# Head of a hybrid decoder step: adaLN modulation in tiles of 128 columns, a PSUM bank each for factors and shifts, low weight parts on VectorE

## The chip, the cores and the metric

One core of one Trainium2 chip runs the whole program. The metric is the time of one execution on the device in microseconds (us). Engines: TensorE (PE, with its weight loads as PEld), VectorE (DVE), ScalarE (ACT), GpSimd (POOL) and SyncE (SP), which here only issues DMAs. Each engine works through a stream of its own in the order written, and waits for other engines by semaphores.

## What is computed

One step of a decoder layer with 1024 new prompt tokens and 32 new sample tokens (8 sequences of 4). The head, where the change lies, is `modulated_input` and the first two column blocks of the product with `w_in`:

```
mod = jax.nn.silu(c) @ w_ada + b_ada
shift, scale, gate = jnp.split(mod, 3, axis=-1)
h = rms_norm(x, g_norm) * (1 + scale[:, None, :]) + shift[:, None, :]
...
u = h @ w_in
```

`c` has 9 rows (one for the prompt, eight for the samples), `w_ada` is 1024 x 3072, `w_in` 1024 x 6468. Behind the head come the remaining projections, an index with the choice of 256 keys per query, retention, sparse attention and the output projection. All products with `h` are made in split precision: an operand is cut into a high part (rounded to the PE's fast fp32 format) and a low part (the rest), and three products are summed: high by high, low of `h` by high of the weight, high of `h` by low of the weight.

## The kernel before

`h` is kept transposed: model columns on the partitions, in 8 tiles `k` of 128 columns, with 1056 tokens beside each other. `XT[:, k]` holds x transposed; `HH[k]` and `HL[k]` are the high and low parts of the modulated tile.

**Loading.** SP issues, in this order: x in nine row tiles; then for each of the `GROUPS` of one or two column tiles the scale columns and the shift columns of `w_ada` (`load_wa`, L329 to L335, 1 MB for a group of two, 512 KB for one), and behind each of the first four groups a quarter (`piece`) of the two first blocks of `w_in` (`ws`, L345). x and `w_ada` share six buffers of 1 MB (`part`, L258).

**Start.** PE transposes x (L307), ACT and DVE evacuate it and sum its squares (`x_block`), DVE makes the inverse root for all tokens in nine small steps (L438 to L446), PE spreads it over the partitions (`spreads`, L452), and ACT copies that into `RB`.

**A tile.** For each tile `k` there is a chain over the engines:
- `modulation(g, o)`, step `m` in the table: PE multiplies silu(c) by the group's `w_ada` columns (L220), in 8 products of 32 rows that fill four row groups; ACT copies the result to SBUF (L388). `o` is 1 for the scale, 0 for the shift.
- `gather(k, o)` (L397): PE sums the four row groups and turns the tile's result into columns in PSUM. All columns of both kinds stand in the tile `Z`; the results of `modulation` stand in the two halves of the tile `M`.
- `factor(k)` (ACT, L406) makes `AA`, the factor of the tile; `scaled(k, 0)` and `scaled(k, 1)` (DVE, L409) multiply the prompt's two halves of `XT[:, k]` by it and by `RB`; `new_scaled` (L412) does it for the 32 sample tokens. This is `scale_tile`, step `z.1`.
- `moved(k)` (ACT, L418) makes `BB`, the shift; `new_moved` (DVE, L415) adds it for the samples; `high(k, 0)`, `high(k, 1)` (ACT, L421) write `HH[k]` with the shift added; `low` (DVE, L424) writes `HL[k]`. This is `shift_tile`, step `z.0`.
- `weight_high` (ACT, L427) and `weight_low` (POOL, L430) split a piece of the two weight blocks; a piece serves two tiles.
- `products` (PE, L243): five matmuls (three of 352 columns, two of 400) for each of the terms 0 (high by high), 1 (low of `h`) and 2 (low of the weight).

The order of all this is written by hand. `on` (L355) ties each instruction behind the one written before it on its engine, and the table `steps` says which pieces of work stand between the terms of each tile:

```
steps = {0: "0 2 1 m21", 1: "0 z21 m20 1a z20 1b 2 m31", 2: "0 z31 1 m30 2a z30 2b", 3: "0 z41 z40 1 2 m51",
         4: "0 z51 m50 1a z50 1b 2", 5: "0 z61 z60 1 2 m71", 6: "0 z71 m70 1a z70 1b 2", 7: "0 1 2"}
```

The factor and the shift of tiles 0 and 1 come ahead of the first product, and tile 1 is modulated before the loop. `idle` (L368) puts matmuls of zeros on PE while it would stand still there. Behind the head the next blocks follow at L227 to L229 (`terms`), with weights split at L212 (ACT) and L213 (DVE, every third on POOL). `prefetch` loads their weights (L206) into the buffers of `ws`, once these are split.

Of the kernel before, what the change touches and what calls it, by code (L numbers as in the profile page):

```python
# [125 lines left out]
def _hybrid_step(ctx, tc, A, outs, dbg):  # L126
# [124 lines left out]
    Z, M = pt(), pt()  # L251
    with ExitStack() as s0:
# [23 lines left out]
        X, pair = {}, [None]  # L276

        def x_load(i):
            t = SEQ[i]
            if i % 2 == 0:  # L280
                pair[0] = part()
            X[t] = pair[0][:, i % 2]
# [93 lines left out]
        rows_, group, turn = {}, {}, [0]
        for g, n in GROUPS:
            group.update({k: g for k in range(g, g + n)})

        def modulation(g, o):  # L380

            n = dict(GROUPS)[g]
            at = 256 * (turn[0] % 2)
            pm = M[:, at:at + 128 * n]
            pe(lambda: ada_rows(pm, lambda c: wa[g, o][:, c]))
            ar = rows_[g, o] = BI[(5, 6, 3, 4)[turn[0] % 4]].bitcast(F32)[:, :128 * n]
# [1 line left out]
            return lambda: sca.copy(ar, pm)  # L388
# [4 lines left out]

        def gather(k, o):

            at = 128 * (k - group[k])
            pe(lambda: nc.tensor.matmul(column(k, o), rows_[group[k], o][:, at:at + 128], C[:, C_S9 + 9 * (1 - o):C_S9 + 9 * (1 - o) + 9], start=True, stop=True))  # L397
# [49 lines left out]
        spread = [pj(), px().rearrange("p a b -> p (a b)")]  # L447

        def spreads(g):
            for o in range(4):  # L450
                i = 1 + 4 * g + o
                last = nc.tensor.matmul(spread[g][:, 128 * o:128 * o + 128], y[:, i:i + 1].to_broadcast([128, 128]), ident, start=True, stop=True)  # L452
            return last

        dve(*held[6:])
# [2 lines left out]
        pe(lambda: spreads(0), lambda: nc.tensor.matmul(own, y[:NS, 0:1].to_broadcast([NS, 128]), ident[:NS, :NS], start=True, stop=True))
        gather(0, 1)
        gather(1, 1)  # L460
        act(lambda: sca.copy(RB[:, :512], spread[0]), factor(0), factor(1))
        pe(lambda: spreads(1))
        act(lambda: sca.copy(RB[:, 512:T], spread[1]))
# [2 lines left out]
        W = [[sp.tile([128, KT, 128], F32R, name="w", bufs=4) for _ in "hl"] for _ in (0, 1)]
        pe(idle(6, 256, spare))
        kept = modulation(0, 0)
        act(kept)
        pe(idle(4, 256, spare))  # L470
        gather(0, 0)
        gather(1, 0)
        pe(idle(8, 256, spare))
        act(moved(0))
        dve(new_moved(0))
        act(weight_high(0, 0), high(0, 0), weight_high(1, 0))
        pool(weight_low(0, 0), weight_low(1, 0))
        dve(lambda: vec.tensor_scalar(HH[0][:, parts[1]], XT[:, 0, parts[1]], shift(0), None, op0=OP.add),
            low(0, 0), low(0, 1))
# [1151 lines left out]
```

## Time and profile before

| what | us |
| --- | --- |
| median of three runs (lowest, highest) | 1107.62 (1106.94, 1108.46) |
| the profiled execution's own time | 1108.76 |
| its span, first to last instruction | 1107.0 |
| DVE busy, ACT busy, POOL busy in the span | 677.0, 468.9, 238.0 |
| first product of the head (L243) starts | 26.07 |
| first product behind the head (L227) starts | 63.61 |

A page of the profile gives the busy time of each engine, lists the costliest groups of instructions, and says what ended the idle time before them. Further views are cut from the same trace: the timeline (start, duration, engine, line, operation, output and input tiles, and in brackets how long the engine had been idle before and what released it), the waits (who waited for whom, in all, how often, longest), stretches of time with the busy time of each engine, and the DMA traffic of a stretch. PEld rows show when PE took up a matmul, which is sharper than the modelled ends of PE rows.

### The profile page before, as it was taken

What the parts mean: (1) busy time and instruction counts of PE and PEld (TensorE: products, weight loads), DVE (VectorE), ACT (ScalarE), POOL (GpSimd) and SP (SyncE); (2) the same over time, 40 slices, a digit from 0 to 9 for tenths busy, and PEclk for the clock granted to TensorE, in tenths of its full rate; (3) what the DMA queues carried; (4) which work ended last, traced back from release to release, by engine and by line L of the source; (5) the groups of instructions that cost most, each with busy time, mean ns of one, the idle gap of its engine ahead of it and who ended that gap; (6) DMA issues with size and microseconds to landing.
All of it is one profiled execution on the core that took longest, in us unless ns stands there. A gap on an engine that the chain in (4) does not pass through costs nothing. (4 is left out here: it accounts for less than half of the span.)

```text
span 1107.0 us, 20368 instructions
## 1 busy us (share of the span) xinstructions
PE 1085.6 (98%) x8081; PEld 986.4 (89%) x8081; DVE 677.0 (61%) x1626; ACT 468.9 (42%) x919; POOL 238.0 (21%) x203
## 2 busy tenths in 40 slices
PE   7999999999999999999999999999999999999996
PEld 6789889899999989999999998887998888898775
DVE  6685348698877878999233222210357767497665
ACT  5475445554554554333244233311336656342111
POOL 0213006113311311020422222244114333000000
PEclk9999999999999999999999999999999999999998
DMA  9643435164344516432886867476798520466431
GB/s 328 189 110 97 122 98 156 47 205 138 92 132 136 175 37 191 142 95 88 287 285 204 239 172 246 130 279 229 256 318 297 182 69 30 138 190 246 160 117 57
DMA packets 149956, 185.63 MB, mean 168 GB/s; under 512 B 18644, under 2 KB 120932, under 8 KB 148772
## 3 DMA queue, kind: packets, MB, share of 16 engines
q1 hardware_dynamic: 139488, 147.81, 42.2%
q0 software_dynamic: 9856, 35.66, 9.8%
q8 instruction: 63, 1.03, 0.4%
q10 hardware_dynamic: 516, 0.86, 0.2%
q14 instruction: 33, 0.27, 0.1%
HBM read 139.34 MB, written 41.17 MB: 163 GB/s over the span
## 5 line engine op out<-in xcount | busy, mean ns | idle before, releaser
L227 PE MATMUL pj<-hh,wh 128*128 128x352 f32 (+1 forms) x1168 | 382.7, 328 | 0.0
L228 PE MATMUL pj<-hl,wh 128*128 128x352 f32 (+1 forms) x1168 | 378.7, 324 | 0.0
L229 PE MATMUL pj<-hh,wl 128*128 128x352 f32 (+1 forms) x1168 | 378.1, 324 | 0.2 <-POOL wl L213 0.2
L227 PEld LDWEIGHTS pj<-hh,wh 128*128 128x128 f32 x1168 | 219.3, 188 | 8.4 <-issue 7.1
L228 PEld LDWEIGHTS pj<-hl,wh 128*128 128x128 f32 x1168 | 219.8, 188 | 6.8 <-issue 6.0
L229 PEld LDWEIGHTS pj<-hh,wl 128*128 128x128 f32 x1168 | 219.4, 188 | 3.8 <-issue 3.2
L997 DVE TENSOR_SCALAR_CACHE_REDUCE eq<-sc,cand 128x896 bf16<-128x896 f32 (+4 forms) x155 | 135.7, 876 | 2.5
L212 ACT CAST wh<-ws 128x1024 fp32r<-128x1024 f32 (+1 forms) x65 | 61.0, 942 | 117.2 <-PE pj L228 88.0
L213 DVE TENSOR_TENSOR wl<-ws,wh 128x1024 fp32r<-128x1024 f32 (+1 forms) x47 | 52.8, 1124 | 41.6 <-ACT wh L212 41.4
L1345 POOL TENSOR_SCALAR lg<-lg,st 128x1024 f32<-128x1024 f32 (+7 forms) x64 | 47.7, 751 | 115.9 <-DVE st L1344 64.9
L213 POOL TENSOR_TENSOR wl<-ws,wh 128x1024 fp32r<-128x1024 f32 x18 | 43.3, 2405 | 93.6 <-ACT wh L212 87.6
L1343 ACT ACTIVATE lg<-lg,st 128x1024 f32<-128x1024 f32 (+7 forms) x64 | 49.4, 774 | 27.6 <-DVE st L1342 26.0
L1215 DVE COPY kt<-str 128x512 f32<-128x512 f32 x32 | 22.1, 691 | 63.3 <-PE str L1213 55.9
L1542 PE MATMUL pj<-woh,MH 128*128 128x512 f32 (+1 forms) x136 | 51.4, 378 | 0.0
L1543 PE MATMUL pj<-wol,MH 128*128 128x512 f32 (+1 forms) x136 | 51.2, 377 | 0.0
L1544 PE MATMUL pj<-woh,ML 128*128 128x512 f32 (+1 forms) x136 | 51.2, 377 | 0.0
L1182 POOL DMA_INDIRECT kv<-in_cache_k,idx x32 | 30.1, 941 | 94.4 <-PE str L1213 85.6
L1215 ACT COPY kt<-str 128x512 f32<-128x512 f32 x32 | 18.8, 588 | 61.9 <-PE str L1213 58.3
L1358 PE MATMUL tr<-C,lg 128*128 128x128 f32 x288 | 43.0, 278 | 1.5 <-ACT pT L1361 0.6
L835 ACT ACTIVATE raw<-pj 128x352 f32<-128x352 f32 x48 | 22.3, 464 | 48.3 <-PE pj L229 41.9
L1182 POOL DMA_INDIRECT kv<-in_cache_v,idx x32 | 31.5, 984 | 52.2 <-PE sx L1243 27.8
L1358 PEld LDWEIGHTS tr<-C,lg 128*128 128x128 f32 x288 | 32.5, 140 | 9.1 <-issue 4.9
(368 smaller groups left out, 1981.1 us busy)
## 6 DMA issues: line engine op xcount, KB each, us to landing
ws<-in_w_in SPq DMA_DIRECT2D x49, 512.0 KB
rot<-in_rot SPq DMA_DIRECT2D x8, 1056.0 KB
TG<-raw SPq DMA_DIRECT2D x15, 528.0 KB
x<-in_w_ada SPq DMA_DIRECT2D x6, 1024.0 KB
wst<-in_w_out SPq DMA_DIRECT2D x12, 512.0 KB
u<-TG SPq DMA_DIRECT2D x8, 528.0 KB
t<-TG SPq DMA_DIRECT2D x8, 528.0 KB
x<-in_x_prompt SPq DMA_DIRECT2D x8, 512.0 KB
```

The costliest lines, as they stand in the source:

```text
L212: nc.scalar.copy(wh[:, :, :n], ws[:, :, :n])
L213: (nc.vector if k == 4 or len(order) % 3 else nc.gpsimd).tensor_sub(wl[:, :, :n], ws[:, :, :n], f32(wh[:, :, :n]))
L227: nc.tensor.matmul(p, wh[:, k], HH[k][:, sl], start=(k == 0), stop=False)
L228: nc.tensor.matmul(p, wh[:, k], HL[k][:, sl], start=False, stop=False)
L229: nc.tensor.matmul(p, wl[:, k], HH[k][:, sl], start=False, stop=(k == KT - 1))
L997: nc.vector.tensor_scalar(junk[:n, :W], sc, thr[:n, j:j + 1], 0.0, op0=op, op1=OP.add, accum_out=cnt[:n, j:j + 1])
L1182: nc.gpsimd.indirect_dma_start(out=t.rearrange("p s c -> p (s c)"), out_offset=None, in_=cache.rearrange("g (r s) h d -> (g r) (s h d)", s ...
L1343: nc.scalar.activation(l, l, AF.Exp, bias=st[:, 2:3], scale=0.125, accum_out=st[:, 3:4])
L1358: step["turned"] = nc.tensor.transpose(x[:, 128 * (j - j0):128 * (j - j0) + 128], lg[:, j % 2, 128 * (j // 2):128 * (j // 2) + 128], ident)
L1542: nc.tensor.matmul(x, MH[:, k, tk], wh[:, k], start=(k == 0), stop=False)
L1543: nc.tensor.matmul(x, MH[:, k, tk], wl[:, k], start=False, stop=False)
L1544: nc.tensor.matmul(x, ML[:, k, tk], wh[:, k], start=False, stop=(k == KT - 1))
```

## The change

`w_ada` is loaded tile by tile in 512 KB for scale and shift each, from eleven buffers of 512 KB; a piece of `w_in` follows the tiles 0, 2, 4 and 5 (`AT`). The results and columns of the scale stand in one PSUM tile, `S[0]`, those of the shift in another, `S[1]`. Only the factor and shift of tile 0 are made ahead of the first product. In the loop both modulations of tile k+2 stand behind the terms of tile k, and scale and shift of tile k+1 directly behind each other. `weight_high` moves from `scale_tile` to `shift_tile`, and `weight_low` from POOL to DVE, behind `low`. Of the `idle` matmuls 4 of 384 columns are left; 18 of 256 go. At the start the second half of tile 0 is scaled from PSUM and not from `RB`, and the held copies of x stand in another order.

```
-GROUPS = ((0, 2), (2, 1), (3, 2), (5, 2), (7, 1))
...
-    Z, M = pt(), pt()
+    S = [pt(), pt()]
...
-        part = lambda: sp.tile([128, 2, D], F32, name="x", bufs=6)
+        part = lambda: sp.tile([128, D], F32, name="x", bufs=11)
...
-        def load_wa(g, n):
+        AT = (0, 2, 4, 5)
+
+        def load_wa(k):
             for o in (1, 0):
-                w = part().rearrange("p a b -> p (a b)")[:, :KT * 128 * n].rearrange("p (k f) -> p k f", k=KT)
-                loads.append(nc.sync.dma_start(w, wcols(A["w_ada"][0], KT, 1024 * o + 128 * g, 128 * n)))
-                wa[g, o] = w
+                w = wa[k, o] = part().rearrange("p (k f) -> p k f", f=128)
+                loads.append(nc.sync.dma_start(w, wcols(A["w_ada"][0], KT, 1024 * o + 128 * k, 128)))
...
-        for j, (g, n) in enumerate(GROUPS):
-            load_wa(g, n)
-            if j < 4:
+        for k in range(KT):
+            load_wa(k)
+            if k in AT:
+                i = AT.index(k)
...
+        def modulation(k, o):
+            pm = S[1 - o][:, :128]
+            pe(lambda: ada_rows(pm, lambda c: wa[k, o][:, c]))
+            ar = rows_[k, o] = BI[(5, 6, 3, 4)[turn[0] % 4]].bitcast(F32)[:, :128]
+            turn[0] += 1
+            act(lambda: sca.copy(ar, pm))
...
         def column(k, o):
-            return Z[:, 18 * k + 9 * (1 - o):18 * k + 9 * (1 - o) + 9]
+            return S[1 - o][:, 256 + 9 * k:265 + 9 * k]
...
         def weight_low(i, j):
-            return lambda: gps.tensor_sub(W[i][1][:, piece[j]], ws[i][:, piece[j]], f32(W[i][0][:, piece[j]]))
+            return lambda: vec.tensor_sub(W[i][1][:, piece[j]], ws[i][:, piece[j]], f32(W[i][0][:, piece[j]]))
...
-        pe(idle(4))
-        kept = modulation(0, 1)
-        act(kept)
+        spare = px().rearrange("p a b -> p (a b)")
+        pe(idle(2, spare))
+        modulation(0, 1)
+        pe(idle(2, spare))
+        gather(0, 1)
+        act(factor(0))
...
+        pe(spreads(0), lambda: nc.tensor.matmul(own, y[:NS, 0:1].to_broadcast([NS, 128]), ident[:NS, :NS], start=True, stop=True))
+        act(lambda: sca.copy(RB[:, :512], spread[0]))
+        modulation(0, 0)
+        pe(spreads(1, (0, 1)))
+        gather(0, 0)
...
+        act(weight_high(0, 0), moved(0))
...
+            scaled(0, 0, RB[:, :512]), new_scaled(0), new_moved(0))
+        pe(spreads(1, (2, 3)))
+        dve(scaled(0, 1, spread[1]))
+        act(high(0, 0), weight_high(1, 0), lambda: sca.copy(RB[:, 512:T], spread[1]))
         dve(lambda: vec.tensor_scalar(HH[0][:, parts[1]], XT[:, 0, parts[1]], shift(0), None, op0=OP.add),
-            low(0, 0), low(0, 1))
...
+            low(0, 0), low(0, 1), weight_low(0, 0), weight_low(1, 0))
+        modulation(1, 1)
...
         def shift_tile(k):
             gather(k, 0)
             act(moved(k))
             dve(new_moved(k))
+            if k in AT:
+                act(*[weight_high(i, AT.index(k)) for i in (0, 1)])
             act(high(k, 0), high(k, 1))
             dve(low(k, 0), low(k, 1))
+            if k in AT:
+                dve(*[weight_low(i, AT.index(k)) for i in (0, 1)])
...
+        steps = ["0a 0b m10 z11 1 z10 2 m21 m20"] + ["0 z%d1 z%d0 1 2 m%d1 m%d0" % (k + 1, k + 1, k + 2, k + 2) for k in range(1, 6)] + ["0a z71 z70 0b 1 2", "0 1 2"]
```

In the new table `0a` is the first of a term's five matmuls and `0b` the other four.

The start on DVE, from the root's application to the sample tokens on. Before (hh_77 and hl_85 are the parts of tile 0, hl_86 one of tile 1):

```order
L464 TENSOR_TENSOR xt<-xt,px 128x8x32
L409 SCALAR_TENSOR_TENSOR xt<-xt,AA,rb 128x512 x2
L412 TENSOR_TENSOR xt<-xt,AA 128x32
L409 SCALAR_TENSOR_TENSOR xt<-xt,AA,rb 128x512 x2
L412 TENSOR_TENSOR xt<-xt,AA 128x32
L415 TENSOR_TENSOR xt<-xt,pt 128x32
L478 TENSOR_SCALAR hh_77<-xt,BB 128x544
L424 SCALAR_TENSOR_TENSOR hl_85<-xt,BB,hh_77 128x512
L424 SCALAR_TENSOR_TENSOR hl_85<-xt,BB,hh_77 128x544
L415 TENSOR_TENSOR xt<-xt,pt 128x32
```

The same place of DVE in the changed kernel, where L401 is `scaled`, L404 `new_scaled`, L407 `new_moved`, L416 `low` and L422 `weight_low`:

```order
L462 TENSOR_TENSOR xt<-xt,px 128x8x32
L401 SCALAR_TENSOR_TENSOR xt<-xt,AA,rb 128x512
L404 TENSOR_TENSOR xt<-xt,AA 128x32
L407 TENSOR_TENSOR xt<-xt,pt 128x32
L401 SCALAR_TENSOR_TENSOR xt<-xt,AA,pj 128x512
L467 TENSOR_SCALAR hh_77<-xt,BB 128x544
L416 SCALAR_TENSOR_TENSOR hl_85<-xt,BB,hh_77 128x512
L416 SCALAR_TENSOR_TENSOR hl_85<-xt,BB,hh_77 128x544
L422 TENSOR_TENSOR w<-ws,w 128x256 x2
L401 SCALAR_TENSOR_TENSOR xt<-xt,AA,rb 128x512 x2
```

Tile 1's scaling (three rows before) has moved behind tile 0's low part, the second half of tile 0 reads PSUM (pj), and two low parts of weights stand in the row.

PE in the step of tile 6 (hh_83, hl_91), before; L220 is the shift's modulation of tile 7, L397 the gathers:

```order
L243 MATMUL pl<-hh_83,w 128x352 x2
L243 MATMUL pj<-hh_83,w 128x352
L243 MATMUL pl<-hh_83,w 128x400 x2
L397 MATMUL pt<-C,bi_99 128x9
L220 MATMUL pt<-x,scT 32x128 x8
L243 MATMUL pl<-hl_91,w 128x352 x2
L243 MATMUL pj<-hl_91,w 128x352
L397 MATMUL pt<-C,bi_100 128x9
L243 MATMUL pl<-hl_91,w 128x400 x2
```

The same step in the changed kernel, from the modulations of tile 7 (L219) behind tile 5 on:

```order
L219 MATMUL pt<-x,scT 32x128 x16
L242 MATMUL pl<-hh_83,w 128x352
L389 MATMUL pt<-C,bi_97 128x9
L389 MATMUL pt<-C,bi_98 128x9
L242 MATMUL pl<-hh_83,w 128x352
L242 MATMUL pj<-hh_83,w 128x352
L242 MATMUL pl<-hh_83,w 128x400 x2
L242 MATMUL pl<-hl_91,w 128x352 x2
L242 MATMUL pj<-hl_91,w 128x352
L242 MATMUL pl<-hl_91,w 128x400 x2
```

Both modulations of tile 7 now stand ahead of tile 6, and both gathers follow each other behind the first matmul.

More of the change, by code (lines that the diff above doesn't have):

```diff
@@ L275, in _hybrid_step, with x_load @@
         size = lambda t: 128 if t < 8 else NS
[L276 to L282, printed above, removed]
+        X = {}
+        def x_load(t):
+            X[t] = part()
             nc.sync.dma_start(X[t][:size(t)], xp[t * 128:t * 128 + 128] if t < 8 else xs)
@@ L362, in on, with idle @@
                 L[engine] = made.ins
-        pe, act, dve, pool = [lambda *fs, e=e: on(e, *fs) for e in "pavg"]
-        vec, sca, gps = nc.vector, nc.scalar, nc.gpsimd
+        pe, act, dve = [lambda *fs, e=e: on(e, *fs) for e in "pav"]
+        vec, sca = nc.vector, nc.scalar
         L["p"], L["a"], L["v"] = [last_on(e) for e in (mybir.EngineType.PE, mybir.EngineType.Activation, mybir.EngineType.DVE)]
-        def idle(n, w=384, out=M):
+        def idle(n, out):
             def run():
                 for i in range(n):
-                    last = nc.tensor.matmul(out[:, 512 - w:], zeros[:, :128], zeros[:, :w], start=True, stop=True)
+                    last = nc.tensor.matmul(out[:, :384], zeros[:, :128], zeros, start=True, stop=True)
                 return last
             return run
[L376 to L386, printed above, removed]
+        rows_, turn = {}, [0]
+        def modulation(k, o):
+            pm = S[1 - o][:, :128]
+            pe(lambda: ada_rows(pm, lambda c: wa[k, o][:, c]))
+            ar = rows_[k, o] = BI[(5, 6, 3, 4)[turn[0] % 4]].bitcast(F32)[:, :128]
             turn[0] += 1
-            return lambda: sca.copy(ar, pm)
+            act(lambda: sca.copy(ar, pm))
         def column(k, o):
-            return Z[:, 18 * k + 9 * (1 - o):18 * k + 9 * (1 - o) + 9]
+            return S[1 - o][:, 256 + 9 * k:265 + 9 * k]
         def gather(k, o):
-            at = 128 * (k - group[k])
-            pe(lambda: nc.tensor.matmul(column(k, o), rows_[group[k], o][:, at:at + 128], C[:, C_S9 + 9 * (1 - o):C_S9 + 9 * (1 - o) + 9], start=True, stop=True))
+            pe(lambda: nc.tensor.matmul(column(k, o), rows_[k, o], C[:, C_S9 + 9 * (1 - o):C_S9 + 9 * (1 - o) + 9], start=True, stop=True))
         halves = (slice(0, 512), slice(512, T))
@@ L446, in _hybrid_step @@
             lambda: vec.scalar_tensor_tensor(y, u, 1.875, y, op0=OP.add, op1=OP.mult))
[L447 to L455, printed above, removed]
-        own = px()[:, 0, :NS]
-        spare = px().rearrange("p a b -> p (a b)")
@@ L458, in _hybrid_step @@
[L458 to L463, printed above, removed]
-        dve(lambda: vec.tensor_tensor(XT[:, :, T:], XT[:, :, T:], own.unsqueeze(1).to_broadcast([128, KT, NS]), op=OP.mult),
-            scaled(0, 0, RB[:, :512]), scaled(0, 1, RB[:, 512:T]), new_scaled(0), scaled(1, 0, RB[:, :512]), scaled(1, 1, RB[:, 512:T]), new_scaled(1))
@@ L466, in _hybrid_step @@
[L466 to L478, printed above, removed]
-            low(0, 0), low(0, 1))
@@ L480, in _hybrid_step, with spreads, run @@
-        act(moved(1))
-        dve(new_moved(1))
-        act(high(1, 0), high(1, 1))
-        dve(low(1, 0), low(1, 1))
+        spread = [pj(), pj()]
+        def spreads(g, os=range(4)):
+            def run():
+                for o in os:
+                    i = 1 + 4 * g + o
+                    last = nc.tensor.matmul(spread[g][:, 128 * o:128 * o + 128], y[:, i:i + 1].to_broadcast([128, 128]), ident, start=True, stop=True)
+                return last
+            return run
+        dve(held[8], held[6], held[7])
@@ L486, in _hybrid_step @@
         ps = ps1.enter_context(tc.tile_pool(name="ps", bufs=1, reuse_waits="tile", space=PSUM))
-        Z, M = pt(), pt()
+        S[:] = pt(), pt()
         banks = first_banks()
-        def put(k, term, some=slice(None)):
-            pe(lambda: Ins(products(W, banks[some], k, term)))
         def scale_tile(k):
@@ L495, in scale_tile @@
             act(factor(k))
-            if k % 2 == 0:
-                act(*[weight_high(i, k // 2) for i in (0, 1)])
-                pool(*[weight_low(i, k // 2) for i in (0, 1)])
             dve(scaled(k, 0, RB[:, :512]), scaled(k, 1, RB[:, 512:T]), new_scaled(k))
```

24 lines of the change are left out of this document (11 added, 13 removed).

## The prediction

> **What bounds the kernel now.** I read the page first, then stretches of time.
>
> ```profile
> span 1107.0 us, 20368 instructions
> ...
> 0.00:64.00 64.00, 55.70 (x445) 44.55 (x446) 44.13 (x89) 35.57 (x79) 10.66 (x13) 0.97 0.75 240
> ...
> PE tr L1358 <- ACT pT L1361: 0.6, 2, 0.3
> ```
>
> The columns of a stretch are its length, busy time of PE, PEld, DVE, ACT and POOL, granted PE clock, DMA share and GB/s. PE is busy for 55.7 of the head's 64 us, so 8.3 of idle lie here; the last row leads the list of PE's waits for other engines behind 63.4 us. PE sets the pace there, and what the head saves should reach the end. The waits of 26 to 63.5 us say what holds PE back there:
>
> ```profile
> DVE xt L409 <- ACT AA L406: 6.2, 6, 1.9
> ACT hh L421 <- DVE xt L415: 4.3, 4, 1.3
> PEld pl L243 <- ACT hh L421: 3.1, 5, 1.0
> ...
> PE pt L397 <- ACT AA L406: 0.9, 2, 0.5
> ```
>
> No row names a DMA. PE waits for the high part, ACT for the sample tokens, DVE for the factor: the chain of a tile. Here it is for tile 7, to the head's end:
>
> ```profile
> 57.53 0.37 PEld L397 LDWEIGHTS pt<-C,bi 128*128 128x128 f32 x2
> 58.03 0.36 ACT L406 ACTIVATE AA<-pt,cols 128x9 f32<-128x9 f32 x1 [1.01 <-PE pt L397]
> 58.42 1.42 DVE L409 SCALAR_TENSOR_TENSOR xt<-xt,AA,rb 128x512 f32<-128x512 f32 x2 [0.74 <-ACT AA L406]
> 59.40 0.26 ACT L418 ACTIVATE BB<-pt,cols 128x1 f32<-128x1 f32 x1 [0.50 <-PE pt L397]
> 59.70 1.36 ACT L421 ACTIVATE hh<-xt,BB 128x512 fp32r<-128x512 f32 x2
> 60.04 0.19 DVE L415 TENSOR_TENSOR xt<-xt,pt 128x32 f32<-128x32 f32 x1
> 60.45 1.45 DVE L424 SCALAR_TENSOR_TENSOR hl<-xt,BB,hh 128x512 fp32r<-128x512 f32 x2 [0.22 <-ACT hh L421]
> 61.11 0.19 PEld L243 LDWEIGHTS pl<-hh,w 128*128 128x128 f32 x1 [0.45 <-ACT hh L421]
> 62.08 2.40 POOL L213 TENSOR_TENSOR wl<-ws,wh 128x1024 fp32r<-128x1024 f32 x1 [6.33 <-ACT wh L212]
> 63.43 0.19 PEld L227 LDWEIGHTS pj<-hh,wh 128*128 128x128 f32 x1
> ```
>
> From the gather at 57.53 to the second high part's end (59.70 + 1.36 = 61.06) pass 3.53 us, and PE takes the tile's second matmul right behind, at 61.11. Other tiles take longer:
>
> ```profile
> 29.74 0.30 PEld L243 LDWEIGHTS pl<-hh,w 128*128 128x128 f32 x2 [0.20 <-issue]
> 30.52 0.37 PEld L397 LDWEIGHTS pt<-C,bi 128*128 128x128 f32 x2
> 31.41 1.89 DVE L409 SCALAR_TENSOR_TENSOR xt<-xt,AA,rb 128x512 f32<-128x512 f32 x2 [1.47 <-ACT AA L406]
> 52.37 0.37 PEld L397 LDWEIGHTS pt<-C,bi 128*128 128x128 f32 x2
> ```
>
> The scaling takes 1.89 us, not 1.42, while POOL makes weight parts. From tile 2's gather (30.52) to tile 7's (57.53) pass 27.01 us, 5.4 a tile; from tile 6's (52.37) alone 5.16.
>
> **Part 1: the tiles' rhythm.** First PE's own work. A term of five matmuls takes 30.52 - 29.74 = 0.78 us. Two modulations of 128 columns in a row exist later, and two gathers at the start:
>
> ```profile
> 232.63 0.81 PEld L220 LDWEIGHTS pj<-ws,scT 128*32 128x32 f32 x32 [0.22 <-issue]
> 233.64 0.19 PEld L227 LDWEIGHTS pj<-hh,wh 128*128 128x128 f32 x1 [0.20 <-issue]
> ...
> 20.50 0.52 PEld L397 LDWEIGHTS pt<-C,bi 128*128 128x128 f32 x4
> 20.94 0.19 PEld L452 LDWEIGHTS px<-C,yy 128*128 128x128 f32 x1
> ```
>
> The pair takes the gap of 0.22 ahead and 233.64 - 232.63 = 1.01, so 1.23 us; the two gathers take 0.44. A tile of the new table is 3 x 0.78 + 0.44 + 1.23 = 4.01 us of PE.
>
> Now the chain with the shift's gather directly behind the scale's: gather at 0, `AA` 0.50 to 0.86, scaling 0.89 to 2.31, samples scaled and shifted by 2.70 (0.19 each, as at 60.04), second high part 2.73 to 3.45. PE takes the second matmul at about 3.5, and after four matmuls (0.63) the next tile's gather: a period of 4.15 us. The first matmul can run at 0.44 + 2 x 0.78 + 1.23 = 3.23, so PE idles some 0.1 us a tile: two limits, 4.01 and 4.15, nearly meet. The separate banks matter here: PE's two waits of L397 on `AA` (up to 0.5 us) were the shift's gather waiting for the factor's read of the shared tile `Z`.
>
> Does DVE fit? It takes 1.42 + 0.19 + 0.19 + 1.45 = 3.25 us a tile, and on four tiles the weights' low parts:
>
> ```profile
> L213 DVE TENSOR_TENSOR wl<-ws,wh 128x512 fp32r<-128x512 f32 x16 | 11.3, 712 | 0.0
> ...
> 62.98 2.57 DVE L213 TENSOR_TENSOR wl<-ws,wh 128x1024 fp32r<-128x1024 f32 x1 [0.81 <-ACT wh L212]
> ```
>
> Half of 0.712 is 0.36 for 128x256; the upper end is a quarter of the 2.57 us pass over 1024 columns, which ran beside POOL's of 62.08: 0.64. With POOL idle I take 0.36, the nearer row: 3.25 + 0.72 = 3.97 us, inside 4.15, so it costs nothing while DVE's wait for the factor covers it. At 0.64 a tile would be 4.53, up to 0.4 too long on four tiles, 1.5 us in all. ACT needs 2 x 0.27 (copies) + 0.36 + 0.26 + 1.36 = 2.5 us a tile, and its weight parts fall into its wait for the scaling. POOL's passes vanish from the loop, and with them the 1.89.
>
> So tile 2's gather to tile 7's: four periods and a last one where `0a` alone stands ahead of the gathers. There PE needs only 3.3 us, but ACT must first finish tile 6's second high part (3.45) and the copy of the factor's row (0.27): 3.75. Sum 4 x 4.15 + 3.75 = 20.35 against 27.01: **-6.65 us**.
>
> **Part 2: the start.**
>
> ```profile
> 18.57 0.17 DVE L446 SCALAR_TENSOR_TENSOR yy<-rb,yy 128x9 f32<-128x9 f32 x1
> 20.27 0.59 ACT L461 COPY rb<-pj 128x512 f32<-128x512 f32 x1 [0.69 <-PE pj L452]
> 25.36 0.72 ACT L421 ACTIVATE hh<-xt,BB 128x512 fp32r<-128x512 f32 x1
> 25.42 0.50 DVE L478 TENSOR_SCALAR hh<-xt,BB 128x544 fp32r<-128x544 f32 x1
> 26.30 1.17 PE L243 MATMUL pl<-hh,w 128*128 128x352 f32 x6
> 29.17 0.38 PEld L220 LDWEIGHTS pt<-x,scT 128*32 128x32 f32 x16 [0.26 <-issue]
> 29.88 0.27 ACT L388 COPY bi<-pt 128x128 f32<-128x128 f32 x1 [0.76 <-PE pt L220]
> ...
> L1545 DVE SCALAR_TENSOR_TENSOR xo<-pj,gb 128x512 f32<-128x512 f32 x15 | 10.2, 686 | 14.8 <-PE pj L1544 13.3 <-DMA out<-xo 1.3
> ```
>
> The root (18.74) still comes when it did, the copy into `RB` at about 20.1. The shift of tile 0 now sits on PE at 20.3: from a modulation (29.17) to its copy's end (30.15) pass 0.98 us, gather and `BB` take 0.8 (a gather's 0.50 as ahead of `AA`, and 0.26), so `BB` is there at 22.1 and the high part at 22.1 to 22.85, where it began at 25.36. The second half waits for the second spread (22.4), scaling from PSUM 0.75 (between 0.69 as in the last row, another pass from PSUM, and 0.95, half of 1.89) and DVE's high part 0.50: second matmul at 23.75 against 26.30. But four matmuls (0.63), a lone modulation (29.74 - 29.17 and a gap, 0.82), two lone gathers (0.35 each), two terms and a pair (1.23) come before tile 1: 23.75 + 0.63 + 0.82 + 0.70 + 1.56 + 1.23 = 28.7, and tile 2's gather at 29.5 against 30.52: **-1.0 us**. The removed zero matmuls stood in waits for ACT and DVE, so their going saves nothing beside that. Of the moved DVE copies, the one that frees the second spread's bank goes first; they end when they did, and cost nothing.
>
> **Part 3: the end.** PE's first low-weight matmul behind the head waited for POOL's 2.40 us (62.08), which followed ACT's split, which followed tile 7's high part: 62.08 + 2.40 = 64.48, 3.4 us behind 61.06. That tail stays.
>
> **Part 4: the loads.** Packets per 3 us with 1 KB pieces (14 to 17 us) and with 512-byte pieces (22 to 25 us), and when the first piece of `w_ada` was there:
>
> ```profile
> DMA packets 1033, 1.06 MB, mean 352 GB/s; under 512 B 16, under 2 KB 1028, under 8 KB 1033
> ...
> DMA packets 1775, 0.89 MB, mean 296 GB/s; under 512 B 52, under 2 KB 1775, under 8 KB 1775
> ...
> 18.07 0.59 PEld L220 LDWEIGHTS pt<-x,scT 128*32 128x32 f32 x16 [0.40 <-DMA x<-in_w_ada]
> ```
>
> All of `w_ada` now comes at the lower rate. At 14.0 us x, whose pieces are 4 KB, is over (1,028 of the 1,033 packets behind it are under 2 KB). From there 9.44 MB (8.39 of `w_ada`, 1.05 of `w_in`) take 31.9 us; each landing lags by 1.05 us (1.05 MB at 352 GB/s end at 17.0, PE went on at 18.07). Tile 7's shift lands at 47.0; PE wants it at 48.9 (tile 6's gather at 29.5 + 4 x 4.15 = 46.1, then 0.44, two terms, and the first of the pair). The least slack, tiles 3 and 6, is 1.3 us. The buffers cost no wait: the sixteen loads need eleven, and each later one takes that of an x tile or of a modulation long past. So the loads cost nothing, by a thin cover: 3.99 us per tile against 4.15.
>
> **Sum.** -6.65 - 1.0 = -7.65. No tile of before ran without a small stall that such a sum leaves out; I give back 0.1 a tile: **-7.0 us**. On the profiled run's 1108.76 (span 1107.0) that is 1101.8; the median of the runs is 1.1 lower: **1100.6**.
>
> **Rivals.**
>
> *A cold clock.*
>
> ```profile
> 39.40:42.80 3.40, 2.09 (x12) 1.72 (x12) 2.11 (x4) 2.24 (x6) 0.24 (x1) 1.00 1.11 300
> 42.80:46.20 3.40, 3.40 (x18) 2.55 (x20) 3.14 (x6) 1.63 (x3) 1.91 (x2) 0.53 0.09 29
> ```
>
> After a stretch with 2.09 of 3.40 us busy the clock fell to 0.53 for the next 3.4 us: 0.47 x 3.4 = 1.6 us of work lost, a part of the 27.01; the 20.35 has none such. The new start has fewer fillers; at 22.3 to 25.7 I count 2.3 us of PE work. If that, or a stall in the loop, costs one to three such stretches, the time is 1102.2 to 1105.4. The Trainium skill ("TensorE: Matmul & The Clock Gate", Part 1) says that it takes an idle window of about 3.4 us; by that no fall would come here, but the trace had one at 61% busy.
>
> *Loads set the pace.* At 270 GB/s tile 7's shift lands at 50.0, 1.1 late: 1101.7; at 250, 52.8 and 3.9 late: about 1104.5. **Slower** than before comes from the same place: tile 7's high part ends 2.7 us behind the landing (0.98 + 0.05 + 0.43 + 0.26 + 0.22 + 0.75), so the old 61.06 is missed if the landing is past 58.4, that is under 9.44 MB / 43.3 us = 218 GB/s. At 200 GB/s the landing is at 62.2: +3.8, 1111.4. For it: half as many packets again (6,144 of 12,288 are cut in two) and a slack of 1.3 us. Against: 296 GB/s on just such packets.
>
> The Trainium skill ("DMA: Bandwidth & Descriptors", sections Anatomy of one DMA and Bandwidth) speaks for this rival: batch transfers to 1 MiB or more. By the page's fit of 2.0 us plus the bytes at 436 GB/s, an estimate for sixteen loads one at a time is 51 us where the old ten need 39, and the kernel would be slower. The trace doesn't bear that out: loads of 128 and 512 KB flowed at 22 to 25 us without a gap.
>
> *It doesn't carry.* The head ends earlier, but an index load or a weight block then holds PE; against it speaks that PE's waits behind the head are tiny. 1107.6.
>
> **Chances.** Forecast (1099 to 1102.5) 0.60; cold clock or loads at 250 to 270 (to 1105.4) 0.23; no change within 0.2% (2.2 us, about what a measurement can tell) 0.09; slower 0.08, against faster 0.83. The range leaves out the last two and a bit below: 1098 (no give-back, and the high parts a little quicker) to 1106.
>
> **What would show it.** Right: tile 2's gather near 29.5, gathers 4.1 to 4.3 us apart, tile 7's second high part ending near 54, low weights of 0.36 us on DVE, no wait for `w_ada` after 18 us. Wrong: PE waiting for a DMA, a clock near 0.5, or scaling (DVE) waiting behind `low`.

## The result, and the profile after

The changed kernel takes 1100.66 us (median of 4 runs, 1099.72 to 1101.49) against 1107.28 us of the kernel before beside it (4 runs, 1106.85 to 1108.46): ratio 0.9938, 95% interval 0.9921 to 0.9956. A second set gave 1100.81 us (5 runs), ratio 0.9935, 0.9921 to 0.9948. The profiled execution has a span of 1099.7 us, 7.3 less than before.

The whole and the head's 64 us, in the columns of the prediction's stretches:

```profile
span 1099.7 us, 20540 instructions
...
0.00:64.00 64.00, 55.77 (x556) 48.37 (x557) 48.59 (x106) 41.77 (x98) 2.58 (x5) 1.00 0.83 240
```

POOL's 10.66 us have become 2.58, and the mean clock went from 0.97 to 1.00. PE's waits of 26 to 57.5 us, out of the list of waits:

```profile
DVE xt L401 <- ACT AA L398: 4.8, 6, 1.6
...
PEld pt L219 <- DVE hl L416: 1.3, 1, 1.3
PE pt L219 <- DVE hl L416: 1.1, 1, 1.1
...
PEld pl L242 <- ACT hh L413: 0.9, 3, 0.5
```

The waits of L397 (now L389) on `AA` are gone; a wait of a modulation, L219, has come. Here is the loop on PE's weight loads: L389 the pair of gathers, L219 the modulations, L242 products, L226 and L228 the first weight block behind the head.

```profile
29.10 0.59 PEld L389 LDWEIGHTS pt<-C,bi 128*128 128x128 f32 x4
33.49 0.59 PEld L389 LDWEIGHTS pt<-C,bi 128*128 128x128 f32 x4
38.05 0.59 PEld L389 LDWEIGHTS pt<-C,bi 128*128 128x128 f32 x4
42.24 0.59 PEld L389 LDWEIGHTS pt<-C,bi 128*128 128x128 f32 x4
...
44.84 0.41 PEld L219 LDWEIGHTS pt<-x,scT 128*32 128x32 f32 x16 [0.45 <-ACT hh L413]
46.58 0.41 PEld L219 LDWEIGHTS pt<-x,scT 128*32 128x32 f32 x16 [1.33 <-DVE hl L416]
...
47.96 0.59 PEld L389 LDWEIGHTS pt<-C,bi 128*128 128x128 f32 x4
51.65 0.52 PEld L389 LDWEIGHTS pt<-C,bi 128*128 128x128 f32 x4
...
54.31 0.75 ACT L413 ACTIVATE hh<-xt,BB 128x544 fp32r<-128x544 f32 x1 [0.28 <-DVE xt L407]
...
57.43 0.19 PEld L226 LDWEIGHTS pj<-hh,wh 128*128 128x128 f32 x1
...
58.53 0.19 PEld L228 LDWEIGHTS pj<-hh,wl 128*128 128x128 f32 x1 [0.42 <-POOL wl L212]
```

Tile 2's gather stands 1.42 us earlier (30.52 before), tile 7's 22.55 behind it (27.01 before), the first weight block 5.78 behind that (5.90 before, at 63.43): -1.42 - 4.46 - 0.12 = **-6.00 us**. The periods are 4.39, 4.56, 4.19, 5.72 and 3.69; the fourth holds a wait for tile 6's shift. The row names DVE's low part, but DVE had long finished there; the load is the suspect. The 6.0 us arrive whole at the end. SP's last issue of the output, before and after (ACT's own last one follows 0.20 us later in both):

```profile
1102.04 0.33 SPq L1577 DMA_DIRECT2D out<-xo  x1
```
```profile
1096.05 0.33 SPq L1558 DMA_DIRECT2D out<-xo  x1
```

That is 5.99 apart; the other 1.3 us of the span's 7.3 lie behind it, where the last write lands.

### The profile page after: what moved, and what is told of

It reads as the page before. It is cut to its first block, busy times and chain, and to the rows that moved or that the text cites. A ratio compares the mean times of both kernels' runs of the same rounds, so it can differ in the third digit from the quotient of the medians.

```text
span 1099.7 us, 20540 instructions
## 1 busy us (share of the span) xinstructions
PE 1079.8 (98%) x8159; PEld 984.8 (90%) x8159; DVE 674.9 (61%) x1634; ACT 468.6 (43%) x925; POOL 229.1 (21%) x195
## 3 DMA queue, kind: packets, MB, share of 16 engines
q8 instruction: 64, 1.05, 0.4%
## 5 line engine op out<-in xcount | busy, mean ns | idle before, releaser
L226 PE MATMUL pj<-hh,wh 128*128 128x352 f32 (+1 forms) x1168 | 382.7, 328 | 0.0
L228 PE MATMUL pj<-hh,wl 128*128 128x352 f32 (+1 forms) x1168 | 378.2, 324 | 0.2 <-POOL wl L212 0.2
L226 PEld LDWEIGHTS pj<-hh,wh 128*128 128x128 f32 x1168 | 219.3, 188 | 8.4 <-issue 7.1
L228 PEld LDWEIGHTS pj<-hh,wl 128*128 128x128 f32 x1168 | 219.4, 188 | 3.8 <-issue 3.2
```

The source lines that it names most:

```text
L226: nc.tensor.matmul(p, wh[:, k], HH[k][:, sl], start=(k == 0), stop=False)
L228: nc.tensor.matmul(p, wl[:, k], HH[k][:, sl], start=False, stop=(k == KT - 1))
```

## The experiments

Each run is read in the same three places: tile 2's gather, from there to tile 7's gather, and the first weight block. Single times of one kernel differ by up to 3.3 us (15 runs of the kernel before lay between 1106.91 and 1110.20), so the kernels with one run are compared by the places alone, which do not depend on the tail.

| kernel | tile 2's gather | to tile 7's | first weight block | time, us (runs) |
|---|---|---|---|---|
| before | 30.52 | 27.01 | 63.43 | 1107.28 (4) |
| after | 29.10 | 22.55 | 57.43 | 1100.66 (4) |
| after_again | 29.07 | 21.75 | 56.60 | 1100.81 (5) |
| half_loads | 29.40 | 20.48 | 55.66 | 1099.62 (1) |
| late_piece | 29.16 | 20.69 | 56.00 | 1100.97 (1) |
| old_loads | 32.04 | 20.49 | 58.32 | 1102.58 (1) |
| mixed_loads | 30.89 | 20.49 | 57.15 | 1101.71 (1) |
| pair_factors | 36.86 | 20.47 | 63.11 | 1107.63 (11) |
| pair_factors2 | 30.22 | 21.76 | 57.76 | 1102.02 (5) |
| low_on_pool | 30.17 | 23.81 | 59.77 | 1103.39 (1) |
| one_bank | 29.61 | 26.35 | 61.92 | 1106.36 (1) |
| before_low_dve | 31.64 | 24.61 | 62.14 | 1106.79 (1) |
| before_two_banks | 30.20 | 26.39 | 62.48 | 1108.19 (1) |
| before_filler | 31.72 | 25.87 | 63.48 | 1108.67 (1) |

### What holds the loop: the loads or the work of a tile?

**half_loads**

```
-  dma_start(w, wcols(A["w_ada"][0], KT, 1024 * o + 128 * k, 128))
+  dma_start(w[:, :4], wcols(A["w_ada"][0], 4, 1024 * o + 128 * k, 128))
-  pe(lambda: ada_rows(pm, lambda c: wa[k, o][:, c]))
+  pe(lambda: ada_rows(pm, lambda c: wa[k, o][:, c % 4]))
```

> The changed kernel, but each of the sixteen loads of w_ada fetches only its first four of eight row blocks, and the modulations use these four twice; half of w_ada's rows are left out of the result. It has the same instructions on every engine, in the same order, with 4.2 MB less to load. Theory A, the loads set the pace: in the changed kernel tile 2's gather stands at 29.10 us and tile 7's at 51.65, 22.55 apart where the forecast had 20.35, and PE waited for shifts of tiles 3, 4 and 6. With half the bytes these waits go: 20.4 to 21.0 us from gather to gather, the first weight block's start at 55.4 to 56.0 instead of 57.43, the whole about 1.5 to 2 us shorter. Theory B, the chain of a tile is longer than the forecast's 4.15 us (small stalls between ACT, DVE and PE), and the loads only fill time that was lost anyway: 22 us or more, weight block within 0.5 us of 57.43.

The pairs of gathers in its timeline of PE's weight loads:

```profile
29.40 0.59 PEld L389 LDWEIGHTS pt<-C,bi 128*128 128x128 f32 x4
33.60 0.59 PEld L389 LDWEIGHTS pt<-C,bi 128*128 128x128 f32 x4
37.80 0.59 PEld L389 LDWEIGHTS pt<-C,bi 128*128 128x128 f32 x4
41.99 0.59 PEld L389 LDWEIGHTS pt<-C,bi 128*128 128x128 f32 x4
46.20 0.59 PEld L389 LDWEIGHTS pt<-C,bi 128*128 128x128 f32 x4
49.88 0.52 PEld L389 LDWEIGHTS pt<-C,bi 128*128 128x128 f32 x4
```

Four periods of 4.20 and one of 3.68: theory A. The loop's own pace is 20.48 us, and the loads cost the profiled execution of the change 22.55 - 20.48 = 2.07 us.

The rows of one period, from the gathers at 37.80 to those at 41.99, say what this pace is made of:

```profile
40.21 0.81 PEld L219 LDWEIGHTS pt<-x,scT 128*32 128x32 f32 x32 [0.26 <-issue]
40.53 0.75 ACT L413 ACTIVATE hh<-xt,BB 128x544 fp32r<-128x544 f32 x1 [0.27 <-DVE xt L407]
41.22 0.30 PEld L242 LDWEIGHTS pl<-hh,w 128*128 128x128 f32 x2 [0.20 <-issue]
```

PE waits for no other engine here. Its own work fills the period: gathers 0.51, two terms 0.79 and 0.85, the pair of modulations 0.26 + 1.01 with its gap, and the next tile's first term 0.77, together 4.19. The chain ends beside it: the second high part is there at 40.53 + 0.75 = 41.28, and PE takes up the first two matmuls of the tile from 41.22 on. The two limits meet within a tenth of a microsecond, and no run here shortens one of them alone.

**after_again**: the changed kernel once more.

> The changed kernel once more, for how much the loads' rate differs between executions: in the profiles so far with all of w_ada in 512-byte pieces it was 8.5 to 8.9 MB from 14 to 47 us. If the waits for shifts of tiles 3, 4 and 6 belong to the kernel, tile 2's gather to tile 7's is 22 to 23 us again; if they belong to one execution with slow loads, it is 20.5 to 21.5 us here with 8.8 MB or more by 47 us, and the first weight block starts at 55.5 to 56.5 us.

21.75 us, between the two, with the same wait for tile 6's shift. One row of 14 to 44 us for each execution (the last number is GB/s), first after, then after_again, then late_piece:

```profile
14.00:44.00 30.00, 28.36 (x327) 23.45 (x326) 24.60 (x57) 18.43 (x49) 0.00 (x0) 1.00 1.06 281
```
```profile
14.00:44.00 30.00, 28.80 (x331) 24.06 (x330) 24.95 (x57) 18.80 (x49) 0.00 (x0) 1.00 1.09 288
...
45.76 0.41 PEld L219 LDWEIGHTS pt<-x,scT 128*32 128x32 f32 x16 [1.05 <-DVE hl L416]
```
```profile
14.00:44.00 30.00, 29.44 (x338) 24.68 (x336) 25.35 (x57) 18.58 (x48) 0.00 (x0) 1.00 1.09 289
```

So the waits belong to the kernel, and their size (2.07 and 1.27 us) to the execution: 281 and 288 GB/s.

**late_piece**

```
-  AT = (0, 2, 4, 5)
+  AT = (0, 2, 4, 6)
```

> The changed kernel with the last two pieces of w_in loaded behind tile 6's columns of w_ada instead of tile 5's, and their split and low parts moved with them from tile 5 to tile 6. 262 KB stand less ahead of tile 6's factor and shift, about 0.97 us at the 270 GB/s that flow there. If the shift of tile 6 was late by its load, as I read PE's wait of 1.3 us at 46.6 us, its modulation starts about 0.9 us earlier, tile 7's gather stands at about 50.9 instead of 51.65, and the first weight block starts 0.3 to 0.7 us earlier than 57.43 (DVE has 0.75 us more to do near the end). If DVE's low parts held PE there, as the releaser named in the row says, tile 6's shift is taken at the same time, or earlier only by the 0.75 us that DVE no longer does at tile 5, with the factor's wait unchanged.

With 289 GB/s, as in after_again, and 262 KB less ahead of tile 6's shift, 20.69 us instead of 21.75: 1.06 less, where 0.9 was expected, and no wait of that modulation is left. What it won went again right behind the head. The rows of ACT and PE there:

```profile
54.33 1.06 ACT L211 CAST wh<-ws 128x1024 fp32r<-128x1024 f32 x1 [0.69 <-DMA ws<-in_w_in]
55.90 1.05 ACT L211 CAST wh<-ws 128x1024 fp32r<-128x1024 f32 x1 [0.51 <-DMA ws<-in_w_in]
...
57.34 0.20 PEld L869 LDWEIGHTS pt<-C,kiT 128*128 128x128 f32 x2 [0.97 <-ACT kiT L857]
```

The next weight blocks use the two `ws` buffers whose last raw pieces are now split a tile later, so their loads come late, and PE waits 0.97 us. The weight block begins 0.60 us before after_again's, but SP's last issue of the output stands at 1095.55, and at 1095.13 there: nothing of it reaches the end.

**old_loads** and **mixed_loads** keep the new order of work, and load two tiles' columns at once: all as before, or tile 0 and tile 7 alone and the others in pairs.

```
-  part = lambda: sp.tile([128, D], F32, name="x", bufs=11)
+  part = lambda: sp.tile([128, 2, D], F32, name="x", bufs=6)
-  wcols(A["w_ada"][0], KT, 1024 * o + 128 * k, 128)
+  wcols(A["w_ada"][0], KT, 1024 * o + 128 * k, 128 * n)
+  GROUPS = {0: 2, 2: 1, 3: 2, 5: 2, 7: 1}    # old_loads
+  GROUPS = {0: 1, 1: 2, 3: 2, 5: 2, 7: 1}    # mixed_loads
```

> The changed kernel with the loads of w_ada as they were before: one load for two tiles' columns where there were such, in pieces of 1 KB, into six buffers of 1 MB; the order of the work on the engines stays new. Theory A, small loads pay at the start and cost in the loop: tile 0's factors and shifts come with tile 1's, so the first high part ends about 1.3 us later than 21.47 and tile 2's gather stands about 1 us later than 29.10; but at 350 GB/s the loop has no wait for w_ada, and tile 2's gather to tile 7's is 20.4 to 21.5 us instead of 22.55. First weight block 0 to 1.2 us earlier than 57.43. Theory B, the tile by tile loads are what the change gains by: the loop waits for the larger loads as well, and the block starts later than 57.43 by 1 us or more.

> The changed kernel with tile 0's columns of w_ada loaded alone, those of tiles 1 and 2, 3 and 4, 5 and 6 in pairs (1 KB pieces), tile 7's alone, into six buffers. If the 512-byte pieces cost rate in the loop: tile 2's gather to tile 7's 20.4 to 21.5 us instead of 22.55, tile 1's shift or factor up to 1.2 us late at the start, first weight block about 1 us earlier than 57.43 (0.3 to 1.8). If the pieces' size makes no difference to the rate there (the same bytes by the same time): 22.5 us again, and the block at 57.4 or later.

In both the loop takes 20.49 us, its own pace again; over 14 to 44 us they flowed at 325 and 328 GB/s. The price is at the start. The weight loads of PE there, in old_loads:

```profile
18.65 0.38 PEld L219 LDWEIGHTS pt<-x,scT 128*32 128x32 f32 x16 [1.78 <-DMA x<-in_w_ada]
...
23.11 0.38 PEld L219 LDWEIGHTS pt<-x,scT 128*32 128x32 f32 x16 [1.83 <-DMA x<-in_w_ada]
```

Tile 0's factor comes at 18.65 (16.76 in the changed kernel) and its shift at 23.11 (19.72), so tile 2's gather is 2.94 us late; I had expected 1. Of this 0.69 us is a later root (18.87 against 18.18), so small loads win 2.25 to 2.94 us at the start, and they cost 1.3 to 2.1 in the loop. mixed_loads ends where the change does (57.15 against 57.43 and 56.60).

**pair_factors** and **pair_factors2** were to have both: the first two tiles alone, later the factors in pairs and the shifts alone.

```
+  if o and k > 1:
+      if k % 2 == 0:
+          w = sp.tile([128, KT, 256], F32, name="xf", bufs=2)
+          loads.append(nc.sync.dma_start(w, wcols(A["w_ada"][0], KT, 1024 + 128 * k, 256)))
+          wa[k, 1], wa[k + 1, 1] = w[:, :, :128], w[:, :, 128:]
+      continue
...
+  after.enter_context(tc.issue_after(loads[-1].ins))    # pair_factors2 alone
```

> The changed kernel with the factors' columns of tiles 2 and 3, 4 and 5, 6 and 7 loaded in pairs (1 MB in pieces of 1 KB), the shifts and the first two tiles alone as in the change. Half of the later bytes then flow at about 350 GB/s instead of 285. If the loads' rate in the loop is what the changed kernel loses by, and its small first loads what it wins at the start by: tile 2's gather at 28.9 to 29.7 us, 20.4 to 21.0 us from there to tile 7's, first weight block at 55.3 to 56.2 us, and 1.2 to 2 us less than the changed kernel in the whole. If the pairs make tile 2's factor and shift late: gather of tile 2 up to 1 us later, the loop 20.5 us, the whole 0.5 to 1.5 us less.

> The changed kernel with the factors of tiles 2 and 3, 4 and 5, 6 and 7 loaded in pairs of 1 KB pieces, as in the run before, but with each load held behind the one before it in SP's queue (there the pairs had been issued ahead of tile 0's shift, and PE waited 6.0 us for that) and all in six buffers of 1 MB. By its place in the queue tile 0's shift is there at 19 to 20 us again and tile 2's gather at 28.9 to 29.7 us (up to 30.3 if tile 2's shift, behind one pair more, is late); tile 2's gather to tile 7's is 20.4 to 21.2 us, where the changed kernel had 22.55 and 21.75, the first weight block starts at 55.3 to 56.6 us (57.43 and 56.60 there), and the whole is 0 to 1.5 us below the changed kernel's 1100.8. If it is no better than that, the loads' rate in the loop is not to be bettered by half of the bytes in larger pieces, because what the pairs win later they lose at tile 2.

pair_factors missed: the pairs have buffers of their own, and were issued ahead of tile 0's shift. Its rows, a modulation of PE and two stretches:

```profile
22.40:25.80 3.40, 0.00 (x0) 0.00 (x0) 0.00 (x0) 0.00 (x0) 0.00 (x0) 0.50 1.16 314
25.80:29.20 3.40, 3.33 (x26) 2.80 (x26) 0.19 (x1) 1.37 (x4) 0.00 (x0) 0.50 1.07 274
...
25.86 0.63 PEld L219 LDWEIGHTS pt<-x,scT 128*32 128x32 f32 x16 [5.99 <-DMA x<-in_w_ada]
```

The whole gain is lost: ratio to the kernel before 0.9995 (0.9986 to 1.0004). With the order held (pair_factors2) the ratio is 0.9943 (0.9929 to 0.9956): no better than the change. Tile 2's shift, behind one pair more, held PE for 1.30 us, and tile 6's waits as before. No version here that loads all of `w_ada` beats the changed kernel.

### Which part carries the gain?

**low_on_pool** (the changed kernel, low parts back on POOL)

```
-  vec.tensor_sub(W[i][1][:, piece[j]], ws[i][:, piece[j]], f32(W[i][0][:, piece[j]]))
+  nc.gpsimd.tensor_sub(W[i][1][:, piece[j]], ws[i][:, piece[j]], f32(W[i][0][:, piece[j]]))
```

> The changed kernel with the low parts of the first weights back on POOL, where they were before. Theory A, POOL's passes slow DVE's beside them: the scaling of 128x512 takes 1.89 us instead of 1.42 again on the tiles beside them, and the four pieces cost about 0.5 us each where no load is late: the first weight block starts 1 to 2 us behind 57.43. Theory B, the slower scaling is hidden behind the late loads of the shifts: under 0.5 us later. If moving them to DVE cost more there (0.75 us for a tile's two) than it gave, the block starts earlier than 57.43.

The timeline of DVE, POOL and PE around tile 4's scaling, where POOL works, and after it:

```profile
40.85 1.90 DVE L401 SCALAR_TENSOR_TENSOR xt<-xt,AA,rb 128x512 f32<-128x512 f32 x2 [0.79 <-ACT AA L398]
...
41.34 2.00 POOL L422 TENSOR_TENSOR w<-ws,w 128x256 fp32r<-128x256 f32 x2 [7.79 <-ACT w L419]
...
42.67 0.71 DVE L404 TENSOR_TENSOR xt<-xt,AA 128x32 f32<-128x32 f32 x1
43.49 0.19 DVE L407 TENSOR_TENSOR xt<-xt,pt 128x32 f32<-128x32 f32 x1
...
43.73 0.38 PEld L219 LDWEIGHTS pt<-x,scT 128*32 128x32 f32 x16 [0.98 <-DVE xt L407]
```

Theory A, and larger than expected. Its periods are 5.59, 4.20, 5.16, 5.17 and 3.69: three tiles are 1.39, 0.96 and 0.97 over 4.20, together 3.3 us. Of each tile's 0.97 the scaling gives 0.48, and as much again comes from the small scaling of the samples (0.71 for 0.19); what the first of them has beyond that, 0.4, the rows don't explain. PE's next modulation writes the shifts' bank and waits until DVE has read from it. The late loads hide a part: against the two executions of the change the loop is 1.26 and 2.06 us longer.

**one_bank** (the changed kernel, results in halves of one bank, columns in the other)

```
-  pm = S[1 - o][:, :128]
+  pm = S[1][:, 256 * (turn[0] % 2):256 * (turn[0] % 2) + 128]
-  return S[1 - o][:, 256 + 9 * k:265 + 9 * k]
+  return S[0][:, 256 + 18 * k + 9 * (1 - o):265 + 18 * k + 9 * (1 - o)]
```

> The changed kernel with the modulations' results in halves of one PSUM bank and the gathered columns of both factor and shift in the other, as before the change. Theory A, the separate banks carry a part of the gain: the shift's gather waits until ACT has read the factor, 0.3 to 0.4 us a tile, so the gathers stand 4.5 us apart where no load is late, and the first weight block starts 0.8 to 1.5 us behind 57.43. Theory B, the wait falls into time that PE spends waiting for the loads or the high part anyway: within 0.4 us of 57.43.

PE's waits from 28 to 62 us, and the two waits of a tile in the timeline:

```profile
PEld pt L219 <- ACT bi L381: 4.2, 6, 0.9
PEld pt L389 <- ACT AA L398: 3.3, 6, 0.5
...
41.33 0.30 PEld L389 LDWEIGHTS pt<-C,bi 128*128 128x128 f32 x2 [0.54 <-ACT AA L398]
44.47 0.38 PEld L219 LDWEIGHTS pt<-x,scT 128*32 128x32 f32 x16 [0.65 <-ACT bi L381]
```

The loop takes 26.35 us, 5.87 over the loop's own pace, and the weight block is 4.49 late: three times what theory A expected. Beside the gather's 0.54 for the read of `AA`, the shift's modulation waits 0.65 for the copy of the factor's row; together the 1.2 us by which a tile is longer (5.40 against 4.20). At this pace no load is late.

**before_low_dve** and **before_two_banks** make one part of the change alone in the kernel before.

```
-  gps.tensor_sub(W[i][1][:, piece[j]], ws[i][:, piece[j]], ...)    # before_low_dve
+  vec.tensor_sub(W[i][1][:, piece[j]], ws[i][:, piece[j]], ...)
-  pm = M[:, at:at + 128 * n]                                       # before_two_banks
+  pm = (Z, M)[1 - o][:, :128 * n]
-  return Z[:, 18 * k + 9 * (1 - o):18 * k + 9 * (1 - o) + 9]
+  return (Z, M)[1 - o][:, 256 + 9 * k:265 + 9 * k]
```

> The kernel before with one part of the change alone: the low parts of the first weights on DVE, behind the tiles' own low parts, instead of POOL. Theory A, half of the loop's gain is POOL out of DVE's way: the scaling takes 1.42 us instead of 1.89 on the tiles that had POOL beside them, about 0.5 to 1 us each for three of them, and tile 2's gather to tile 7's falls from 27.01 by 1.5 to 2.5 us; first weight block at 61 to 62 instead of 63.43. Theory B, PE is held by the order of its own work there (shift's modulation behind the gather), and DVE's 0.75 us on top take back what the scaling gains: 26.5 us or more, block within 0.6 us of 63.43.

> The kernel before with another part of the change alone: factors and their columns in one PSUM bank, shifts and theirs in the other, at the old places in the order. Theory A: PE's two waits of its gather for the read of AA go, 0.9 us in all, and the first weight block starts 0.5 to 1 us earlier than 63.43. Theory B, the waits lie beside others and the banks alone do nothing, since the shift is still modulated behind the factor's gather: within 0.3 us of 63.43. If one bank for a modulation's result and its own columns makes a new wait (the next factor's modulation behind the last gather's reader), it is slower, by up to 0.5 us a tile.

The low parts on DVE alone: the scaling takes 1.42 everywhere and the loop 24.61 us, 2.40 less, which is theory A's number. But the clock did not fall in this execution; against the kernel before with a clock that stayed up (25.87, next run) it is 1.26 us less, so the low parts give about half of the 2.40, below theory A's range. The banks alone: 0.62 less in the loop, 0.95 at the weight block, and the gather's waits for `AA` are gone; theory A too. Neither makes the change: without the separate banks the new order's loop (26.35) is as long as the old one's with them (26.39). The new order without both parts, and both parts in the old order, were not run.

### What did the cold clock cost before?

**before_filler**

```
+  fill = pj()
-  2: "0 z31 1 m30 2a z30 2b", 3: "0 z41 z40 1 2 m51"
+  2: "0 z31 1 m30 2a z30 2b f4", 3: "f4 0 z41 z40 1 2 m51"
+  if step[0] == "f":
+      pe(idle(int(step[1]), 256, fill))
```

> The kernel before with eight matmuls of zeros (256 columns each, into a spare bank) on PE around the end of tile 2's and the beginning of tile 3's products, where PE was busy for only 2.09 of 3.40 us before the clock fell to 0.53 at 42.8 to 46.2 us. Theory A, the cold clock was a part of the 27.01 us from tile 2's gather to tile 7's: the clock stays at 1.00 and the 27.01 falls by 1.0 to 1.6 us; then the same part of the change's gain came from keeping PE busy. Theory B, the chain through ACT and DVE sets the tile's pace there and hides the slower PE: the clock stays at 1.00 and the 27.01 falls by less than 0.5 us.

The two stretches around 42.8 us:

```profile
39.40:42.80 3.40, 3.19 (x22) 2.57 (x22) 1.63 (x3) 1.96 (x4) 0.00 (x0) 1.00 1.09 295
42.80:46.20 3.40, 2.95 (x27) 2.38 (x29) 2.66 (x5) 1.84 (x5) 2.15 (x2) 1.00 0.12 37
```

The clock stays at 1.00, and the loop takes 25.87 us, 1.14 less: theory A. The 1.14 us lie in one period: from the gather at 41.33 to the one at 47.66 pass 6.33 us before, 5.18 here (42.54 to 47.72), and the other four periods agree within 0.01. So about 1.1 of the 4.46 us that the change wins in the loop is the clock. That the zeros kept it up is argued from one execution of each: in before_low_dve it stayed at 1.00 without them. The weight block is not earlier (63.48), because the start was 1.20 us later in this execution; the kernels of the old order started between 30.20 and 31.72.

## Why the prediction was right, point by point

The time came out as forecast (1100.6 against 1100.66). The mechanism was right with one exception, the loads; that the sum still agrees to 0.1 us is luck, as the terms below show.

- **Part 1, the rhythm: right, with PE's own work too small.** 20.35 us forecast, 20.47 to 20.49 in four kernels whose loads were in time: 4.15 was 4.20, 3.75 was 3.68. The forecast had PE at 4.01 us a tile, idle for 0.1 until the second high part came; PE's own work is 4.19 (third term 0.85 for 0.78, gathers 0.51 for 0.44, pair 1.27 for 1.23), and it doesn't wait. The chain, forecast at 4.15, ends beside it, so the number held. Low parts take 0.75 us for two on DVE (2 x 0.36 forecast), and the scaling 1.42 everywhere. Two reasons for the change were under-priced: POOL also slowed the small scaling, and the shared banks would have held the paired modulations besides the gathers. Neither changes the sum, which counted the new table without them.
- **Part 4, "the loads cost nothing": wrong, and the step that failed.** They cost 2.07 us (1.27 in the second execution). Two numbers were too good. The rate was taken from one stretch of 3 us (296 GB/s); over 14 to 44 us it was 281 and 288. And the lag of 1.05 us was that of the first load. Tile 6's shift is the end of 8.39 MB; in the changed kernel 30 x 281 = 8.44 MB had moved by 44.0, and PE got it at 46.58, so up to 2.7 us behind the bytes (some of those counted may be tile 7's, whose loads had been issued by then). The forecast landing was 14.0 + 28.3 + 1.05 = 43.4: about 1.5 of the 3.2 us between are the rate, 1.7 the landing. The rival "loads set the pace" was thus partly true, at tile 6 rather than tile 7. The Trainium skill ("DMA: Bandwidth & Descriptors", section Bandwidth) advises to batch loads to 1 MiB or more; its measured table, like the fit that the prediction used, is of loads issued from GpSimd, and these are issued by SP. For the loop the advice is what the runs show (old_loads and mixed_loads have no wait there), for the start the opposite (2.94 and 1.79 us later). The runs don't tell the size of a load from the length of its pieces.
- **The give-back of 0.65** was named small stalls. There were none: 4.19 to 4.21 where the loads were in time. The loads took its place, and more.
- **Part 2, the start: right.** -1.42 against -1.0 by the clock. The root was forecast "when it did", but ended at 18.18, 0.56 earlier, and the products began earlier with it:

```profile
18.01 0.17 DVE L441 SCALAR_TENSOR_TENSOR yy<-rb,yy 128x9 f32<-128x9 f32 x1
...
23.01 0.59 PE L242 MATMUL pl<-hh,w 128*128 128x352 f32 x2
...
28.32 0.30 PEld L242 LDWEIGHTS pl<-hh,w 128*128 128x128 f32 x2 [0.20 <-ACT hh L413]
```

  Tile 1's first product stands at 28.32 (forecast 28.7). From the root's end to tile 2's gather pass 11.78 us in before and 11.70 in before_filler, 10.92 in after and 10.76 in after_again: the change itself gives 0.8 to 1.0. The root's 0.56 lies inside the scatter of executions (it ended between 17.97 and 20.02 us in kernels of the old order, 18.18 and 19.69 in those of the new).
- **Part 3, the end: right in the head, incomplete behind it.** The last high part ends at 55.06, the low weights begin at 58.53, 3.47 later (3.4 forecast). But the last write landed 1.3 us sooner behind its issue than before, which nothing in the forecast had. The other traces have it too: from SP's last issue to the span's end pass 3.65 to 4.03 us in all ten of the new order, 4.93 to 4.96 in three of the four of the old, 4.03 in before_low_dve. From the weight block to that issue there is no such difference (1038.2 to 1039.6 us and 1038.5 to 1039.0). Why the write lands sooner is open.
- **The sum.** Forecast -6.65 - 1.0 + 0.65 = -7.0. Measured on the two profiles: -4.46 - 1.42 - 0.12 = -6.0, and -1.3 at the last write. By cause: the loop without its loads -6.53, the loads +2.07, the start -0.86, an earlier root -0.56, the end -0.12, the last write -1.3. The loads' unforeseen cost was paid by the give-back of 0.65, by a root that came early, and by a write that nobody had in the sum. Without that write the median would have been about 1102, in the upper part of the forecast's own range.
- **A cold clock** did not come: 1.00 throughout the loop. That it fell before cost 1.1 us (the prediction said 1.6).
- **It doesn't carry**: it does, 5.99 of 6.00 us at the last issue.

## What to carry to other kernels

When a loop is shortened until it nearly meets its loads, take the loads' rate from a stretch as long as the loop, and the lag from a late load, not from the first. Small loads help where the first tile waits and cost where the stream must keep up; both prices have to be added. Parts of one change may be worth little alone (banks alone 0.6 us in the loop, all but the banks 0.7) and most of the gain together (undone alone, the banks cost 3.8 to 4.6 us in the loop), so undoing a part and doing it alone answer different questions.

## What the runs showed of the hardware that was not expected

- Beside POOL's subtraction of 128x256, DVE's product of 128x32 took 0.71 us instead of 0.19, and the two scalings 1.90 instead of 1.42. The product ended at 42.67 + 0.71 = 43.38, just behind POOL's two subtractions (41.34 + 2.00 = 43.34). The Trainium skill ("SBUF — State Buffer", section SBUF: two separate sides) says that DVE and GpSimd share a pair of ports under an exclusive lock, also when a DVE operation has two inputs in SBUF and GpSimd's reads SBUF. The trace agrees: the product has two inputs in SBUF, and ended when POOL did. Taken one by one, the instructions alternate: the first scaling, begun before POOL, took 0.75 us; POOL's first subtraction 0.87 (41.34 to 42.21); the second scaling, begun at 41.52, 1.23; POOL's second subtraction, begun at 42.16, 1.18; then the product.
- Landings fell behind the bytes: 1.05 us for the first load of the kernel before, up to 2.7 for tile 6's shift in the changed one.
- In pair_factors, after 5.99 us without work, the clock stayed at 0.50 through the next 3.4 us, in which PE was busy for 3.33. There an idle stretch came first; in the kernel before the fall followed a stretch with PE 61% busy. The busy share alone doesn't tell when it falls: it fell behind 2.55 of 3.40 us in before_two_banks (37.9 to 41.3), and not behind 2.39 in before_low_dve (39.6 to 43.0) or 2.26 in low_on_pool (32.8 to 36.2).
